# Three pinned queue orders around the norms: gate products and mask loads behind the power on GpSimd, gate weights' low parts behind the statistics on VectorE

## The chip, the core and the metric

The kernel runs on one core of one Trainium2 chip. The engines are called here as the profile calls them: PE is TensorE, DVE is VectorE, ACT is ScalarE, POOL is GpSimd, SP is SyncE, which issues most of the DMAs. The metric is the device time of one execution in microseconds (us).

## The reference

Two blocks run one after the other on 256 tokens of width 1024. The first has two layers, each with an attention, a short convolution and a state-space scan side by side, and it also carries 256 context tokens through its first layer. Its sublayers end in a gated norm of their output, which is added to the stream:

```python
y = jnp.concatenate([y_att, y_sc, y_ssd], axis=-1) @ p['w_out']
x = x + g1 * _rms_norm(y, p['g_post_mix'])
...
f = jnp.square(jax.nn.relu(h @ p['w_ff1'])) @ p['w_ff2']
return x + gate * _rms_norm(f, p['g_post_ffn'])
```

The second block has two layers, one with a dilated and one with a plain window attention, both masked to a band. Each layer ends like this:

```python
x = layer_norm(DEEPNORM_ALPHA * x + h, ln_g[i], ln_b[i])
gate = jax.nn.sigmoid((x @ ple_w_gate[i]).astype(jnp.float32))
x = x.astype(jnp.float32) + gate * (p[i] @ ple_w_proj[i]).astype(jnp.float32)
```

## The kernel before

The tokens lie in tiles of 128 partitions. `xt[0]` and `xt[1]` are the context's two tiles, `xt[2]` and `xt[3]` those of the stream; each is two halves of 512 columns. A tile's post-norm runs alone, and tiles go in pairs.

A matrix product in float32 is made of three PE matmuls of rounded parts (`mm3`, L212). `split` makes the parts: ACT casts the value to its high part (L226) and DVE, or for every second part of the activations POOL, subtracts it from the value to get the low part (L227). A weight comes by a DMA that SP issues into a tile `raw` (`wblk`, L180 in the profile), and `wh` and `wl` are its high and low parts; a few `raw` tiles go round, so a new DMA waits until an older tile's `wl` is made.

`rpow` (L167, L168) makes the factor of a norm on POOL, with two tiny instructions: an addition of epsilon, and the power −1/2. `postnorm` (L424 and after) squares and sums a tile's two halves on ACT (L431), multiplies the halves by the gate (L432: first half on POOL, second on DVE), calls `rpow`, and adds the product times the factor to the stream on DVE (L435). `normed` (L406, L410) does the next norm: squares on ACT, `rpow`, and a scaling `q` on DVE. `modulated` (L420, L424) transposes `q` on PE, scales the transposed tile `tp` on DVE, and splits it into the parts `u`.

`load_mask` (L1020 and after) loads the mask of a window attention in two halves, with a DMA that POOL's queue issues (L1023) and a cast on POOL (L1024) for each. `second` (L1229 and after) ends a layer of the second block: the out-projection's result is added to the stream (L1245), its statistics are taken (L1246) and joined (L1250), `rpow` makes the factor, two passes normalize it (L1253, L1254), PE transposes it (L1002), and the gate's product follows, with weights from `wblk`.

A scheduler decides the order of the instructions of each engine: it walks the traced program with a simulated timeline and takes what it expects to be ready first, within what the data and the buffers allow. An engine then runs its instructions in that order, one behind the other. Two helpers bind the scheduler. `keep_in_program_order` holds an instruction behind the one that was traced before it on its engine. `issue_after(x)` holds all that is traced inside it behind `x` on the engine of `x`.

Of the kernel before, what the change touches and what calls it, by code (L numbers as in the profile page):

```python
# [13 lines left out]
ALU = mybir.AluOpType  # L14
# [4 lines left out]
KT = D // P  # L19
# [45 lines left out]
def body(ctx, tc, A, out):  # L65
    nc = tc.nc
    PE, ACT, DVE, POOL, SP = nc.tensor, nc.scalar, nc.vector, nc.gpsimd, nc.sync
# [15 lines left out]
    def nm(s):  # L83
        count[0] += 1
        return f"{s}{count[0]}"
# [84 lines left out]
    def wblk(src, segs, k0=0, nk=KT, keep=0, tag="u"):  # L170

        W = sum(w for _, w in segs)
        per = min(1024 // W, nk)
        v = src.rearrange("(k p) n -> p k n", p=P)
        got = []
        for k in range(0, nk, per):
            r = raw.tile([P, 1024], F32, tag="raw", name=nm("raw"))[:, 0:per * W].rearrange("p (k n) -> p k n", k=per)
            o = 0
            for c0, w in segs:
                SP.dma_start(r[:, :, o:o + w], v[:, k0 + k:k0 + k + per, c0:c0 + w])  # L180
                o += w
            if k >= nk - keep:
                for q in range(per):
                    h, l = B(tag, F32R)[:, 0:W], B(tag, F32R)[:, 0:W]
                    split(r[:, q, :], h, l)
                    got.append((h, l))
                continue
            n = min(512 // W, per)
            for a in range(0, per, n):
                h = wh.tile([P, 512], F32R, tag="wh", name=nm("wh"))[:, 0:n * W]  # L190
                l = wl.tile([P, 512], F32R, tag="wl", name=nm("wl"))[:, 0:n * W]
                split(r[:, a:a + n, :].rearrange("p k n -> p (k n)"), h, l)
                for q in range(n):
                    got.append((h[:, q * W:(q + 1) * W], l[:, q * W:(q + 1) * W]))
        return got
# [86 lines left out]
    cols, halves = [None, None], [None, None]  # L282
# [144 lines left out]
    def postnorm(t, halves, gate):  # L427

        s2, rs, r = S(2), S(1), [R(), R()]
        for hf in range(2):  # L430
            ACT.activation(R(), halves[hf], AF.Square, scale=1.0 / 32, accum_out=s2[:, hf:hf + 1])  # L431
            (DVE if hf else POOL).tensor_tensor(r[hf], halves[hf], gate[hf], ALU.mult)  # L432
        rpow(rs, s2[:, 0:1], s2[:, 1:2], EPS)
        for hf in range(2):
            DVE.scalar_tensor_tensor(xt[t][hf], r[hf], rs, xt[t][hf], ALU.mult, ALU.add)  # L435
# [583 lines left out]
    def load_mask(n):  # L1019
        m = C([P, 5, 256], "c_mask", BF16, tag="c_tri")[:, 0:4, :].rearrange("p (s a) c -> p s (a c)", s=2)  # L1020
        for s in range(2):
            r = R()
            POOL.dma_start(r, A[n][:, s * 512:(s + 1) * 512])  # L1023
            POOL.tensor_copy(m[:, s, :], r)  # L1024
        return m

    def gated(po, z, pattern):
# [203 lines left out]
    def second(i, oT, pp, fill, done):  # L1231
        w_out = A["a_w_out_2" if i == 0 else "b_w_out_2"][0]
        lg, lb = [U(), U()], [U(), U()]
        for hf in range(2):
            brow(lg[hf], A["ln_g_2"][i, 512 * hf:512 * hf + 512])
            brow(lb[hf], A["ln_b_2"][i, 512 * hf:512 * hf + 512])
        st = [S(12), S(12)]
        hT, transpose = xT()
        for n in range(2):
            W = wblk(w_out, [(512 * n, 512)])  # L1240
            for t in range(2):
                x = xt[2 + t]
                ps = AN()
                mm3(ps, tok(oT, t, W))
                DVE.scalar_tensor_tensor(x[n], x[n], ALPHA, ps, ALU.mult, ALU.add)  # L1245
                DVE.bn_stats(st[t][:, 6 * n:6 * n + 6], x[n])  # L1246
        for t in range(2):
            x = xt[2 + t]
            mv, rs = S(2), S(1)
            DVE.bn_aggr(mv, st[t])  # L1250
            rpow(rs, mv[:, 1:2], None, LN_EPS)
            for n in range(2):
                DVE.scalar_tensor_tensor(x[n], x[n], mv[:, 0:1], lg[n], ALU.subtract, ALU.mult)  # L1253
                DVE.scalar_tensor_tensor(x[n], x[n], rs, lb[n], ALU.mult, ALU.add)  # L1254
            transpose(t)
        W = [wblk(A["ple_w_gate_2"][i], [(512 * n, 512)], keep=(0 if n else KT)) for n in range(2)]
        got = None
        for t in range(2):
            x = xt[2 + t]
            for n in range(2):  # L1260
                ps = AN()
                mm3(ps, tok(hT, t, W[n]))
                e = R()
                ACT.activation(e, ps, AF.Tanh, scale=0.5)
                DVE.scalar_tensor_tensor(e, e, 1.0, pp[t][n], ALU.add, ALU.mult)
                DVE.tensor_tensor(x[n], x[n], e, ALU.add)
                if i == 1:
                    SP.dma_start(out[0, t * P:(t + 1) * P, 512 * n:512 * n + 512], x[n])
            done(t)
            if t == 0:  # L1270
                got = fill()
        return got
# [97 lines left out]
```

## Time and profile before

| | us |
|---|---|
| median of three runs (lowest, highest) | 1543.17 (1542.04, 1545.42) |
| profiled execution, its own time | 1537.98 |
| its span | 1535.9 |
| PE busy in the span | 1470.2 (96%) |
| DVE busy | 1036.4 (67%) |
| ACT busy | 740.4 (48%) |
| POOL busy | 308.2 (20%) |
| mean granted clock of PE, share of full speed | 0.986 |

A time on the profile's timeline counts from the start of the span. PE is busy for all but 65.7 us of it, so a change of order can win only where PE stands, and it can lose wherever it makes PE stand longer.

### The profile page before, as it was taken

How to read it: one execution, taken by the hardware profiler on the slowest of the kernel's cores; microseconds unless marked ns; L12 is line 12 of the kernel's file. 1: busy time of each engine (PE TensorE's matmuls, PEld its weight loads, DVE VectorE, ACT ScalarE, POOL GpSimd, SP SyncE). 2: the span in 40 equal slices, each digit the busy share in tenths (PEclk: the TensorE clock that was granted, in tenths of full speed). 3: DMA queues.
4: the chain of work that ended last, by engine and by line, in shares of the span. 5: the costliest groups of instructions: out<-in, count | busy, mean ns of one | idle time of the engine just before them, and what ended most of it. 6: DMA issues, size and time to landing. Idle time of an engine off the chain costs nothing.

```text
span 1535.9 us, 23433 instructions
## 1 busy us (share of the span) xinstructions
PE 1470.2 (96%) x8417; PEld 1215.3 (79%) x8417; DVE 1036.4 (67%) x2057; ACT 740.4 (48%) x1594; POOL 308.2 (20%) x356
## 2 busy tenths in 40 slices
PE   6997999999999999998899899999999999999998
PEld 4766678888878888878797689997888889878886
DVE  3559556478597557478776756676876786567866
ACT  3433345564233333255556654565566457445663
POOL 1225201150001111034331301112310320021110
PEclk9998999999999999999999999999999999999999
DMA  9854622325366546334423546555436550645442
GB/s 294 266 182 153 219 84 88 97 66 195 123 219 206 180 152 200 109 83 135 132 76 117 165 139 213 188 195 169 153 107 203 162 179 15 219 139 180 138 149 69
DMA packets 131687, 236.51 MB, mean 154 GB/s; under 512 B 12624, under 2 KB 31251, under 8 KB 131571
## 3 DMA queue, kind: packets, MB, share of 16 engines
q1 hardware_dynamic: 130688, 233.46, 47.0%
q0 software_dynamic: 704, 1.50, 0.3%
q8 instruction: 66, 1.08, 0.3%
q14 instruction: 50, 0.41, 0.1%
q10 hardware_dynamic: 179, 0.06, 0.0%
HBM read 233.87 MB, written 1.11 MB: 153 GB/s over the span
## 4 chain that ended last, share of the span: by engine, by line
PE 84%; DVE 7%; DMA 4%; issue 2%; ACT 2%; POOL 1%; SPq 0%; ACTq 0%; DVEq 0%; POOLq 0%
PE sc L212 47%; PE mm L212 20%; PE tp L459 3%; DVE wl L227 2%; PE fl L303 2%; DMA raw<-in_w_mod_dram 1%; DMA raw<-in_ple_w_gate_dram 1%; PE fl L212 1%; DMA raw<-in_w_in_dram 1%; PE sc L793 1%; PE mm L639 1%; PE sc L1083 1%; PE sc L634 1%; DVE u L782 1%; PE sc L1108 1%
## 5 line engine op out<-in xcount | busy, mean ns | idle before, releaser
L227 DVE TENSOR_TENSOR wl<-raw,wh 128x512 fp32r<-128x512 f32 (+1 forms) x606 | 421.2, 731 | 141.1 <-ACT wh L226 138.1
L226 ACT CAST wh<-raw 128x512 fp32r<-128x512 f32 (+1 forms) x606 | 359.2, 620 | 307.0 <-PE sc L212 104.5
L212 PE MATMUL sc<-wh,u 128*128 128x512 f32 (+2 forms) x1424 | 458.6, 389 | 3.5 <-DVE r L505 2.0
L212 PEld LDWEIGHTS sc<-wh,u 128*128 128x128 f32 x1424 | 265.4, 189 | 58.8 <-ACT p L226 2.2
L212 PE MATMUL sc<-wl,u 128*128 128x512 f32 (+2 forms) x712 | 274.6, 387 | 0.1
L212 PE MATMUL sc<-u,wh 128*128 128x256 f32 (+1 forms) x1072 | 265.1, 336 | 1.8 <-ACT wh L226 1.1
L212 PE MATMUL mm<-wh,u 128*128 128x512 f32 (+1 forms) x648 | 219.3, 395 | 1.0 <-ACT u L226 1.0
L212 PEld LDWEIGHTS sc<-u,wh 128*128 128x128 f32 x1072 | 184.0, 191 | 24.5 <-issue 2.0
L212 PE MATMUL sc<-u,wl 128*128 128x256 f32 (+1 forms) x536 | 178.0, 335 | 0.0
L212 PEld LDWEIGHTS sc<-wl,u 128*128 128x128 f32 x712 | 134.6, 189 | 24.8 <-DVE wl L227 0.5
L949 POOL TENSOR_TENSOR r<-r 128x256 f32<-128x256 f32 (+1 forms) x60 | 64.3, 1073 | 420.1 <-ACT r L947 380.2
L212 PEld LDWEIGHTS mm<-wh,u 128*128 128x128 f32 x648 | 122.2, 190 | 26.1 <-ACT u L226 1.7
L212 PE MATMUL mm<-wl,u 128*128 128x512 f32 (+1 forms) x324 | 127.2, 393 | 0.0
L212 PE MATMUL mm<-u,wh 128*128 128x256 f32 (+1 forms) x512 | 117.6, 317 | 1.1 <-ACT wh L226 1.0
L212 PEld LDWEIGHTS sc<-u,wl 128*128 128x128 f32 x536 | 102.0, 191 | 9.6
L342 DVE SCALAR_TENSOR_TENSOR q<-raw,c_sT,q 128x512 f32<-128x512 f32 x112 | 85.0, 788 | 13.8 <-DMA raw<-in_w_mod_dram 13.2
L212 PEld LDWEIGHTS mm<-u,wh 128*128 128x128 f32 x512 | 86.1, 191 | 9.2 <-issue 1.7
L212 PE MATMUL mm<-u,wl 128*128 128x256 f32 (+1 forms) x256 | 80.4, 314 | 0.0
L950 DVE TENSOR_TENSOR u<-r,u 128x256 fp32r<-128x256 f32 (+1 forms) x60 | 33.6, 561 | 63.0 <-POOL r L949 60.7
L1016 POOL TENSOR_TENSOR r<-r,r 128x512 f32<-128x512 f32 (+1 forms) x30 | 44.6, 1491 | 151.4 <-DVE r L1014 151.3
L212 PEld LDWEIGHTS mm<-wl,u 128*128 128x128 f32 x324 | 61.5, 190 | 12.5 <-issue 0.8
L227 POOL TENSOR_TENSOR u<-r,u 128x256 fp32r<-128x256 f32 (+1 forms) x48 | 38.2, 801 | 119.3 <-ACT u L226 119.0
(318 smaller groups left out, 1984.7 us busy)
## 6 DMA issues: line engine op xcount, KB each, us to landing
raw<-in_w_ff_dram SPq DMA_DIRECT2D x128, 512.0 KB, 4.5
raw<-in_w_mod_dram SPq DMA_DIRECT2D x80, 512.0 KB, 4.5
raw<-in_a_w_in_dram SPq DMA_DIRECT2D x80, 512.0 KB, 3.9
raw<-in_w_in_dram SPq DMA_DIRECT2D x32, 512.0 KB, 5.1
raw<-in_b_w_in_dram SPq DMA_DIRECT2D x18, 512.0 KB, 4.6
raw<-in_w_mod_dram SPq DMA_DIRECT2D x32, 256.0 KB, 5.2
raw<-in_w_out_dram SPq DMA_DIRECT2D x16, 512.0 KB, 3.8
raw<-in_ple_w_gate_dram SPq DMA_DIRECT2D x16, 512.0 KB, 3.9
```

Of the source, the lines that this page charges most:

```text
L212: PE.matmul(ps, s, m, start=(i == 0), stop=(i == n - 1))
L226: ACT.copy(h, src)
L227: (eng or DVE).tensor_tensor(l, src, f(h), ALU.subtract)
L303: PE.matmul(ps[32 * g:32 * g + 32, :], sT[:, k + q, :], rs[g // per][:, q, w * (g % per):w * (g % per) + w], start=(k + q == 0), stop=(k + ...
L342: DVE.scalar_tensor_tensor(a, r[:, q, :], w, a, ALU.mult, ALU.add)
L459: PE.transpose(tp[:, b * P:(b + 1) * P], p[:, b * P:(b + 1) * P], ident)
L634: PE.matmul(ps[:, b * P:(b + 1) * P], qT[t][:, hs], kT[b][:, hs], start=True, stop=True, skip_group_check=True)
L639: PE.matmul(po[64 * e:64 * e + 64, hp * P:(hp + 1) * P], V[b // 2][:, 256 * (b % 2) + 64 * h:256 * (b % 2) + 64 * h + 64], pT[e][:, b * P: ...
L782: DVE.tensor_scalar(o, o, cs[:, t, c:c + 1], 0.0, ALU.subtract, ALU.min)
L949: POOL.tensor_tensor(f2[:, a:b], r[:, a:b], r[:, a:b], ALU.mult)
L950: DVE.tensor_tensor(l, f2[:, a:b], f(h), ALU.subtract)
L1016: POOL.tensor_tensor(a[:, 0:w], a[:, 0:w], b[:, 0:w], ALU.add)
```

## The change

It computes the same with the same instructions. Three places of the code bind the scheduler that did not before. The product on POOL of a `postnorm` is held behind what was traced before it on POOL: for the second tile of a pair that is the first tile's power, and for the first tile of the context's pair it is the last of the POOL subtractions of the stream's `modulated`. The mask's DMAs and casts are held in the order in which they are written, behind the power that was traced before them. In `second`, all that the gate's weights need on DVE is held behind the first tile's joined statistics.

```diff
--- before.py
+++ after.py
@@ -429,7 +429,10 @@
         s2, rs, r = S(2), S(1), [R(), R()]
         for hf in range(2):
             ACT.activation(R(), halves[hf], AF.Square, scale=1.0 / 32, accum_out=s2[:, hf:hf + 1])
-            (DVE if hf else POOL).tensor_tensor(r[hf], halves[hf], gate[hf], ALU.mult)
+            ins = (DVE if hf else POOL).tensor_tensor(r[hf], halves[hf], gate[hf], ALU.mult)
+            if hf == 0:
+
+                tc.keep_in_program_order(ins)
         rpow(rs, s2[:, 0:1], s2[:, 1:2], EPS)
         for hf in range(2):
             DVE.scalar_tensor_tensor(xt[t][hf], r[hf], rs, xt[t][hf], ALU.mult, ALU.add)
@@ -1020,8 +1023,8 @@
         m = C([P, 5, 256], "c_mask", BF16, tag="c_tri")[:, 0:4, :].rearrange("p (s a) c -> p s (a c)", s=2)
         for s in range(2):
             r = R()
-            POOL.dma_start(r, A[n][:, s * 512:(s + 1) * 512])
-            POOL.tensor_copy(m[:, s, :], r)
+            tc.keep_in_program_order(POOL.dma_start(r, A[n][:, s * 512:(s + 1) * 512]))
+            tc.keep_in_program_order(POOL.tensor_copy(m[:, s, :], r))
         return m
 
     def gated(po, z, pattern):
@@ -1244,16 +1247,20 @@
                 mm3(ps, tok(oT, t, W))
                 DVE.scalar_tensor_tensor(x[n], x[n], ALPHA, ps, ALU.mult, ALU.add)
                 DVE.bn_stats(st[t][:, 6 * n:6 * n + 6], x[n])
+        agg = []
         for t in range(2):
             x = xt[2 + t]
             mv, rs = S(2), S(1)
-            DVE.bn_aggr(mv, st[t])
+            ins = DVE.bn_aggr(mv, st[t])
+            agg.append(ins.ins)
             rpow(rs, mv[:, 1:2], None, LN_EPS)
             for n in range(2):
                 DVE.scalar_tensor_tensor(x[n], x[n], mv[:, 0:1], lg[n], ALU.subtract, ALU.mult)
                 DVE.scalar_tensor_tensor(x[n], x[n], rs, lb[n], ALU.mult, ALU.add)
             transpose(t)
-        W = [wblk(A["ple_w_gate_2"][i], [(512 * n, 512)], keep=(0 if n else KT)) for n in range(2)]
+
+        with tc.issue_after(agg[0]):
+            W = [wblk(A["ple_w_gate_2"][i], [(512 * n, 512)], keep=(0 if n else KT)) for n in range(2)]
         got = None
         for t in range(2):
             x = xt[2 + t]
```

Lines below L432 stand three lower after the change, those below L1250 four or five.

**POOL, out-projection of the first layer, the context's pair of tiles.** `r_3027` and `r_3066` are the two tiles' products, `s_3026` and `s_3065` their factors, `u_2611` a low part of the stream's activations. Before:

```order
L432 TENSOR_TENSOR r_3027<-u_2773,q_2637 128x512
L167 TENSOR_SCALAR s_3026<-s_3025 128x1
L432 TENSOR_TENSOR r_3066<-u_2800,q_2637 128x512
L168 TENSOR_TENSOR s_3026<-s_3026,c_mhalf_99 128x1
L167 TENSOR_SCALAR s_3065<-s_3064 128x1
L227 TENSOR_TENSOR u_2611<-r_2996,u_2610 128x256
L168 TENSOR_TENSOR s_3065<-s_3065,c_mhalf_99 128x1
```

After:

```order
L227 TENSOR_TENSOR u_2611<-r_2996,u_2610 128x256
L432 TENSOR_TENSOR r_3027<-u_2773,q_2637 128x512
L167 TENSOR_SCALAR s_3026<-s_3025 128x1
L168 TENSOR_TENSOR s_3026<-s_3026,c_mhalf_99 128x1
L432 TENSOR_TENSOR r_3066<-u_2800,q_2637 128x512
L167 TENSOR_SCALAR s_3065<-s_3064 128x1
L168 TENSOR_TENSOR s_3065<-s_3065,c_mhalf_99 128x1
```

The subtraction `u_2611` has come to the head, and the first tile's power now stands ahead of the second tile's product.

**ACT, the same place.** `s_3025` and `s_3064` gather the two tiles' squares, `sc_3000` is a half of the first tile, `u_2608` and `u_2610` are high parts of the stream's activations. Before:

```order
L431 ACTIVATE r_3029,s_3025<-u_2773 128x512
L431 ACTIVATE r_3032,s_3025<-sc_3000 128x512
L226 CAST u_2608<-r_2989 128x256
L431 ACTIVATE r_3068,s_3064<-u_2800 128x512
L431 ACTIVATE r_3071,s_3064<-sc_3039 128x512
L226 CAST u_2610<-r_2996 128x256
```

After:

```order
L431 ACTIVATE r_3029,s_3025<-u_2773 128x512
L226 CAST u_2608<-r_2989 128x256
L226 CAST u_2610<-r_2996 128x256
L431 ACTIVATE r_3032,s_3025<-sc_3000 128x512
L431 ACTIVATE r_3068,s_3064<-u_2800 128x512
L431 ACTIVATE r_3071,s_3064<-sc_3039 128x512
```

The two casts, of which `u_2610` feeds the subtraction `u_2611`, now stand ahead of the square of the first tile's second half. At the second layer's out-projection the cast `u_8101` and one of a weight have moved ahead of such a square in the same way, the subtraction `u_8101` ahead of the product on POOL, and two weight subtractions ahead of the tile's L435 on DVE.

**POOL, end of the second layer's feed-forward.** `r_10494` and `r_10536` are the products, `s_10493` and `s_10535` the factors, the rest is the first attention mask. Before:

```order
L432 TENSOR_TENSOR r_10494<-u_8757,q_8463 128x512
L167 TENSOR_SCALAR s_10493<-s_10492 128x1
L432 TENSOR_TENSOR r_10536<-u_8772,q_8463 128x512
L168 TENSOR_TENSOR s_10493<-s_10493,c_mhalf_99 128x1
L1023 DMA r_10585<-in_mask_a_dram 128x512
L1023 DMA r_10588<-in_mask_a_dram 128x512
L167 TENSOR_SCALAR s_10535<-s_10534 128x1
L168 TENSOR_TENSOR s_10535<-s_10535,c_mhalf_99 128x1
L1024 CAST c_mask_10584<-r_10585 128x512
L1024 CAST c_mask_10584<-r_10588 128x512
```

After:

```order
L432 TENSOR_TENSOR r_10494<-u_8757,q_8463 128x512
L167 TENSOR_SCALAR s_10493<-s_10492 128x1
L168 TENSOR_TENSOR s_10493<-s_10493,c_mhalf_99 128x1
L432 TENSOR_TENSOR r_10536<-u_8772,q_8463 128x512
L167 TENSOR_SCALAR s_10535<-s_10534 128x1
L168 TENSOR_TENSOR s_10535<-s_10535,c_mhalf_99 128x1
L1026 DMA r_10585<-in_mask_a_dram 128x512
L1027 CAST c_mask_10584<-r_10585 128x512
L1026 DMA r_10588<-in_mask_a_dram 128x512
L1027 CAST c_mask_10584<-r_10588 128x512
```

The first power stands ahead of the second product, and both mask DMAs stand behind both powers, the second of them behind the first cast.

**DVE, second layer norm of the second block.** `x_111` is a half of the first tile, `s_15524` its joined statistics, `wl_15625` and `wl_15629` low parts of gate weights. Before:

```order
L227 TENSOR_TENSOR wl_15625<-raw_15622,wh_15624 128x512
L227 TENSOR_TENSOR wl_15629<-raw_15622,wh_15628 128x512
L1245 SCALAR_TENSOR_TENSOR x_111<-x_111,mm_15470 128x512
L1246 BN_STATS s_15326<-x_111 128x6
L1250 BN_AGGR s_15524<-s_15326 128x2
L1253 SCALAR_TENSOR_TENSOR x_110<-x_110,s_15524,u_15318 128x512
```

After:

```order
L1248 SCALAR_TENSOR_TENSOR x_111<-x_111,mm_15470 128x512
L1249 BN_STATS s_15326<-x_111 128x6
L1254 BN_AGGR s_15524<-s_15326 128x2
L227 TENSOR_TENSOR wl_15625<-raw_15622,wh_15624 128x512
L227 TENSOR_TENSOR wl_15629<-raw_15622,wh_15628 128x512
L1258 SCALAR_TENSOR_TENSOR x_110<-x_110,s_15524,u_15318 128x512
```

The two subtractions have gone from ahead of the tile's last addition to behind its joined statistics. At the first layer norm they moved only behind the joined statistics, since the addition and its statistics stood ahead of them already.

## Rows read from the trace of the kernel before

**Rows 1.** The page: busy time of the engines, share, instructions.
```profile
PE 1470.2 (96%) x8417; PEld 1215.3 (79%) x8417; DVE 1036.4 (67%) x2057; ACT 740.4 (48%) x1594; POOL 308.2 (20%) x356
```

**Rows 2.** Timeline of PE: start, us, instructions, [idle before, releaser].
```profile
321.43 0.41 PE L420 MATMUL tp<-c_ident,q 128*128 128x128 f32 x2 [1.18 <-DVE q L410]
...
699.28 0.41 PE L420 MATMUL tp<-c_ident,q 128*128 128x128 f32 x2 [1.44 <-DVE q L410]
...
864.69 0.50 PE L212 MATMUL mm<-u,u 128*128 128x512 f32 x1 [1.33 <-DVE u L227]
...
1051.31 0.44 PE L985 MATMUL tp<-c_ident,x 128*128 128x128 f32 x2 [1.68 <-DVE x L435]
...
1371.63 0.55 PE L1002 MATMUL tp<-c_ident,x 128*128 128x128 f32 x3 [0.72 <-DVE x L1254]
...
1506.12 0.60 PE L1002 MATMUL tp<-c_ident,x 128*128 128x128 f32 x2 [1.13 <-DVE u L227]
```

**Rows 3.** Windows: stretch, length, busy us (count) by engine, PEclk, DMA share, GB/s.
```profile
1052.30:1055.70 3.40, 3.40 (x9) 2.53 (x9) 0.54 (x2) 0.02 (x1) 0.70 (x2) 0.50 0.02 7
1056.00:1059.40 3.40, 3.40 (x18) 2.75 (x17) 1.51 (x3) 2.03 (x5) 0.00 (x0) 1.00 0.00 0
```

**Rows 4.** Timeline of POOL, out-projection, second pair of tiles.
```profile
313.89 0.30 POOL L167 TENSOR_SCALAR s<-s 128x1 f32<-128x1 f32 x1
...
314.27 1.30 POOL L432 TENSOR_TENSOR r<-u,q 128x512 f32<-128x512 f32 x1
...
315.53 0.74 POOL L168 TENSOR_TENSOR s<-s,c_mhalf 128x1 f32<-128x1 f32 x1
...
317.28 1.10 POOL L227 TENSOR_TENSOR u<-r,u 128x256 fp32r<-128x256 f32 x1
```

**Rows 5.** Timeline of ACT, the same place.
```profile
312.27 0.58 ACT L431 ACTIVATE r<-sc 128x512 f32<-128x512 f32 x1
...
313.47 0.41 ACT L226 CAST u<-r 128x256 fp32r<-128x256 f32 x1 [0.53 <-DVE r L424]
```

**Rows 6.** Timeline of DVE, the same place.
```profile
318.93 1.42 DVE L435 SCALAR_TENSOR_TENSOR u<-r,s,u 128x512 f32<-128x512 f32 x2 [1.15 <-POOL s L168]
...
322.53 0.88 DVE L410 TENSOR_SCALAR q<-u,s 128x512 f32<-128x512 f32 x2 [0.69 <-POOL s L168]
```

**Rows 7.** Timeline of POOL, out-projection of the second layer.
```profile
861.57 1.01 POOL L168 TENSOR_TENSOR s<-s,c_mhalf 128x1 f32<-128x1 f32 x1
...
865.36 1.85 POOL L167 TENSOR_SCALAR s<-s 128x1 f32<-128x1 f32 x1 [2.77 <-ACT r L406]
```

**Rows 8.** Timeline of ACT, the same place.
```profile
860.83 2.18 ACT L226 CAST u<-raw 128x512 fp32r<-128x512 f32 x4
```

**Rows 9.** Timeline of POOL, end of the second layer's feed-forward.
```profile
1045.36 1.30 POOL L432 TENSOR_TENSOR r<-u,q 128x512 f32<-128x512 f32 x1
...
1046.62 1.00 POOL L168 TENSOR_TENSOR s<-s,c_mhalf 128x1 f32<-128x1 f32 x1
...
1047.58 1.17 POOL L1023 DMA_DIRECT2D r<-in_mask_a_dram  x2
```

**Rows 10.** Timeline of DVE, the same place.
```profile
1045.64 2.17 DVE L227 TENSOR_TENSOR wl<-raw,wh 128x512 fp32r<-128x512 f32 x2
...
1050.50 1.41 DVE L435 SCALAR_TENSOR_TENSOR x<-r,s,x 128x512 f32<-128x512 f32 x2 [0.77 <-POOL s L168]
```

**Rows 11.** Timeline of DVE, first layer norm of the second block.
```profile
1367.50 1.29 DVE L227 TENSOR_TENSOR wl<-raw,wh 128x512 fp32r<-128x512 f32 x2 [1.93 <-ACT wh L226]
...
1370.82 1.42 DVE L1254 SCALAR_TENSOR_TENSOR x<-x,s,u 128x512 f32<-128x512 f32 x2 [0.46 <-POOL s L168]
```

**Rows 12.** Timeline of DVE, second layer norm.
```profile
1497.74 1.29 DVE L227 TENSOR_TENSOR wl<-raw,wh 128x512 fp32r<-128x512 f32 x2 [3.62 <-ACT wh L226]
...
1500.64 1.41 DVE L1253 SCALAR_TENSOR_TENSOR x<-x,s,u 128x512 f32<-128x512 f32 x2
```

**Rows 13.** Timeline of SP's queue, second layer norm: DMA issues.
```profile
1499.07 6.46 SPq L180 DMA_DIRECT2D raw<-in_ple_w_gate_dram  x2
```


## The prediction

> **What bounds the kernel now.** I read the page's busy times first: PE works for 1470.2 us [rows 1] of a span of 1535.9 us, and DVE, the next engine, for 67% of it. So PE bounds the kernel, and only the 65.7 us in which it stands can be won. The next view is PE's timeline at the three pinned places, with what ended its waits. The reader is to see that at each of them PE does stand, for one or two microseconds, and waits for the end of a norm [rows 2]: for the scaled tile `q` (1.18 us at 321.43, 1.44 us at 699.28), for the stream `x` after a post-norm (1.68 us at 1051.31), for a normalized `x` (0.72 us at 1371.63), or for a low part `u` (1.33 us at 864.69, 1.13 us at 1506.12). Such a stop can cost more than itself: from 1052.3 to 1055.7 PE ran at a granted clock of 0.50, its lower level of 1.2 GHz, right after it had stood at 1051.31. It began 9 instructions there, against 18 in an equally long stretch at 1.00 soon after [rows 3]. Half of 3.4 us, 1.7 us, is what such a stretch costs.
>
> The third view is the timelines of POOL, ACT and DVE at each place, held against the new order. No instruction and no DMA is added or removed, so every term is a shift of the end of a norm.
>
> **What is the price of a product behind the power.** A product on POOL takes 1.30 us [rows 4], the power 0.74 us [rows 4] to 1.01 us [rows 7]. Before the change the second product stands between the first tile's addition of epsilon (over at 314.19) and its power (315.53), 1.3 us in all [rows 4]. The change takes these away from the first tile. But the product is still needed for the second tile, and it now starts when DVE starts the first tile's L435. What DVE and POOL do to each other at such a time is seen at the other product: two subtractions on DVE that start at 1045.64, while the product runs until 1046.66 [rows 9], take 2.17 us [rows 10], and a pair with no POOL work beside it 1.29 us [rows 11]. So 0.88 us go to the overlap. The other way round, POOL's tiny addition took 1.85 us at 865.36, beside a run of such subtractions on DVE [rows 7], where another took 0.30 us [rows 4]: 1.55 us. One of the two engines pays about a microsecond each time.
>
> The Trainium skill (SBUF — State Buffer, section "Who interferes with whom") has a rule that speaks against the change here: GpSimd and a VectorE instruction with two SBUF inputs share a port, and the one that issues first keeps it for its whole instruction while the other is fully blocked. By it the moved product would cost up to its whole length, 1.30 us, at each place, more than the 0.88 us of the row. The rows agree that one waits for the other; which of them gets the port first behind a power, no row of before shows.
>
> **First layer's out-projection.** Of its two pairs the first has no wait of PE's behind it, and counts as nothing: PE has matmuls of the other tokens to do there. In the context's pair POOL begins with `u_2611`, which needs the cast `u_2610`. On ACT that cast and the one ahead of it stand before the square that began at 312.27; the first of them could begin only at 313.47, since it waited for DVE [rows 5]. Two casts of 0.41 us end at about 314.3, the square of 0.58 us at about 314.9, where before it ended at 312.85. On POOL: `u_2611` from 314.3 (it took 1.10 us) to about 315.3, the first product to 316.6, the addition and the power 0.30 + 0.74 + 0.1 us between them to 317.7. Before, the power ended at 316.27 [rows 4]. The first tile is 1.4 us late although a product was taken out of its way, because two other things were put there. Behind this power come the second product and the second factor: 317.7 + 1.30 + 1.14 = 320.1, if nothing stops the product, against the 318.93 at which the second tile's L435 began upon its factor [rows 6]: 1.2 us late. If the product waits for the L435 pair, 1.42 us [rows 6], it is 2.6 us. Then `q`, which began at 322.53 upon its factor [rows 6], is as late, and PE has nothing else: it stood there already. I take the middle, **+1.9** (1.2 to 2.6).
>
> **First layer's feed-forward end.** The same two edits meet the same pattern in the context's pair, but here the new order also puts about 30 matmuls of the next layer ahead of the transposes for which PE waited 1.44 us [rows 2], and weight subtractions ahead of L435, so that raw tiles come free sooner. The gain is at most that wait, −1.4; the loss is at most what the first place loses, +2.6. The middle, rounded down since the matmuls cover a part: **+0.5**.
>
> **Second layer's out-projection.** `u_8101` and a weight's cast stand ahead of the square, which so waits for two casts. In the row of four the first began at 860.83 and each took a quarter of 2.18 us [rows 8], so the square ends about 862.2, the product 862.7, the power (1.01 us) about 864.0; before, it ended at 861.57 + 1.01 = 862.58 [rows 7]. So L435 is 1.4 us late. The two weight subtractions that now stand ahead of it fill part of this, and they are what PE waits for at 864.69, 1.33 us. Five matmuls also go ahead of the transposes. PE can thus break even or better, −0.5 as I bound it; the worst is L435's 1.4 us and another hold of POOL's addition of 1.55 us, +2.95. I take **+1.2**.
>
> **Second layer's feed-forward end, with the mask.** Here the edit does most of what it can: the power moves up to 1045.36, where the product began, and the mask's DMA issues, 1.17 us of POOL from 1047.58, leave the second factor's way [rows 9]. But on DVE the two subtractions, whose second ends at 1047.81, stand ahead of the first tile's L435 [rows 10], so that tile was not held by its power. The second was: L435 at 1050.50 waited 0.77 us for its factor [rows 10]. That wait, and with it the clock's 1.7 us, is the most that can be won: −2.5. Against it the second product now starts at about 1046.1 among DVE's subtractions. If it is put off to DVE's first L435 (about 1048), it ends near 1050, and with addition and power near 1051.4: 0.9 us late. Between −2.5 and +0.9 I take **+0.2**, since the row of 865.36 shows POOL as the one that waits behind subtractions. The mask itself is first used far later; its later DMA costs nothing here. The second mask's load stands behind a norm in both orders, and is free as well.
>
> **First layer norm.** The joined statistics no longer wait behind the two subtractions that begin at 1367.50 upon a cast, so POOL's factor is ready early and DVE's 0.46 us before L1254 [rows 11] goes. L1253 still waits behind them. PE's transposes come 0.46 us earlier at best, with the joining's own time at most 0.7: **−0.4** (−0.7 to 0).
>
> **Second layer norm.** The subtractions could begin at 1497.74, upon their cast, and ended at 1499.03; what lies between that and 1500.64 [rows 12], 1.6 us of addition and statistics, now goes ahead of them, partly into DVE's wait of 3.62 us. SP issues the next raw tile at 1499.07, as soon as they are over [rows 13]; it goes out up to 1.6 us later, and the casts and low parts behind it come later too. In return L1254 follows without its wait. Bounds: +1.6, and −2.8 if PE's 1.13 us [rows 2] and a slow stretch of 1.7 us go. I take **+0.4**.
>
> **The sum:** 1.9 + 0.5 + 1.2 + 0.2 − 0.4 + 0.4 = +3.8 us. The profiled execution took 1537.98 us, so it would take 1541.8; that execution is 5.2 us below the median of 1543.17, on which I put the same shift: **1547.0**. About 0.2%, 3.1 us, is what a measurement of this kernel can tell from no change.
>
> **The rivals.**
> *Absorbed.* The late factors are covered, since PE's order is rearranged with them: the 30 matmuls and the five take the place of the waits. With the lower bounds of the two places that have such matmuls: 1.9 − 1.4 − 0.5 + 0.2 − 0.4 + 0.4 = +0.2, 1543.4. For it: PE has much ready work at both. Against it: at 321.43 nothing covers.
> *Faster.* PE's stops at 1051.31 and 1506.12 become so short that the clock isn't lowered after them. It decides at the second product of the feed-forward's end: if POOL gets it done before DVE's first L435, −2.5 there, and with −2.5 at the second layer norm, −0.5 at the first, +1.2 at the out-projection and nothing elsewhere −4.3, 1538.9. For it: both DMA issues really leave. Against it: DVE's subtractions stand at just that time.
> *Locked.* Each moved product waits for a whole pair on DVE or makes it wait. It decides at the same instant, behind a power: the upper bounds 2.6 + 2.6 + 2.95 + 0.9 with −0.4 and 0.4 give +9, 1552.2. That is the skill's rule carried through, as far as rows have shown it.
>
> **Chances.** The forecast as worked out 0.36, absorbed 0.35, faster 0.19, locked 0.10. The forecast and locked are slower by over 0.2%: 0.46; same 0.35; faster 0.19. The range leaves out the locked case and a half of the faster one: 1540.0 to 1550.5.
>
> **What would show it.** In the changed profile the first tile's power in the context's pair should end near 317.7 on before's scale, about 1.4 us late, with PE's wait for `q` and those right behind it longer by 1.9 us in sum; the second product of each pair should lie beside L435, one of them stretched. At 1051 PE's wait should stay near 1.7 us and the clock should still fall behind it. The forecast is wrong if the product slips in beside DVE at no cost, if ACT makes the two casts without delaying the square, or if the transposes moved behind matmuls leave PE no wait at all.

## The result, and the profile after

The change made the kernel slower: 1551.21 us against 1543.17 (medians of five runs). The ratio on record is 1.0067 with an interval of 1.0051 to 1.0084, so 8 to 13 us; the quotient of the two medians, 1.0052, lies at its lower end. The forecast was slower too, but +3.8 us, and 1551.21 lies above the range. The profiled execution took 1551.21 us, its span is 1549.3 us, and on the page PE is the engine to look at [rows 1]:

```profile
PE 1475.2 (95%) x8417; PEld 1217.9 (79%) x8417; DVE 1039.6 (67%) x2057; ACT 740.9 (48%) x1594; POOL 302.4 (20%) x356
```

PE stands for 74.1 us instead of 65.7, and is busy for 5.0 us more with the same 8417 instructions. Where this happens is seen by cutting both traces at the same matmuls, counted along PE. The next two views are windows, columns as in [rows 3], each line a stretch: the first 65 us, the first layer's out-projection, its feed-forward's end with what follows, the second layer's out-projection, its feed-forward's end, and the two layer norms. Before:

```profile
4.54:70.11 65.57, 53.21 (x444) 38.44 (x444) 31.34 (x80) 26.20 (x65) 15.91 (x28) 0.97 0.93 304
310.21:345.42 35.21, 31.95 (x232) 29.71 (x231) 25.14 (x47) 21.69 (x56) 19.55 (x25) 0.95 0.15 50
670.28:790.18 119.90, 106.84 (x732) 96.03 (x730) 97.76 (x229) 65.78 (x169) 47.98 (x62) 0.96 0.34 103
853.30:910.18 56.88, 53.79 (x250) 42.49 (x250) 41.42 (x77) 33.57 (x72) 11.07 (x13) 0.97 0.47 149
1045.03:1090.31 45.28, 42.85 (x196) 34.46 (x195) 32.33 (x56) 22.62 (x45) 13.58 (x14) 0.96 0.47 141
1365.31:1415.40 50.09, 46.43 (x227) 37.68 (x225) 37.09 (x70) 24.93 (x54) 10.44 (x9) 1.00 0.44 149
1490.21:1530.44 40.23, 38.79 (x170) 31.12 (x168) 28.76 (x50) 14.14 (x29) 3.40 (x4) 0.96 0.28 92
```

After:

```profile
4.54:73.02 68.48, 52.64 (x444) 38.30 (x445) 31.19 (x80) 26.25 (x65) 16.01 (x28) 0.98 0.90 296
313.05:348.85 35.80, 31.37 (x233) 29.80 (x231) 24.90 (x47) 21.86 (x56) 18.53 (x25) 0.95 0.15 49
674.31:801.50 127.19, 109.35 (x732) 98.47 (x731) 100.25 (x231) 66.89 (x171) 47.60 (x63) 0.93 0.33 97
864.57:923.70 59.13, 55.67 (x250) 43.05 (x251) 41.78 (x77) 33.54 (x72) 9.86 (x13) 0.94 0.44 143
1058.57:1103.22 44.65, 42.86 (x196) 34.51 (x195) 32.47 (x56) 22.71 (x45) 14.07 (x14) 0.96 0.49 144
1378.23:1429.40 51.17, 47.86 (x227) 38.82 (x226) 36.79 (x70) 24.92 (x54) 9.59 (x9) 0.97 0.44 147
1504.20:1543.81 39.61, 38.05 (x170) 29.64 (x168) 28.53 (x50) 14.24 (x29) 2.62 (x4) 1.00 0.29 94
```

Length less PE's busy time is the time that PE stands. The first stretch is 2.9 us longer although no engine's order differs there; that is not the change, and it makes the two profiled spans 13.4 us apart where the timed ratio says about 10. Of the others one stands out, the third: 119.90 us became 127.19, +7.3. PE stands 17.84 us there instead of 13.06, and its clock is 0.93 instead of 0.96, which makes the same 732 matmuls 2.5 us longer. The out-projections have +0.6 and +2.25, the second feed-forward's end −0.6, the layer norms +1.1 and −0.6.

Over the first 240 matmuls of the third stretch (56.5 us, before 47.6) PE stands 12.1 us instead of 7.3, so all of its longer standing lies there. Its four largest waits from 688 to 730 us, by line (total, times, longest):

```profile
PE sc L212 <- ACT u L226: 2.5, 1, 2.5
PE mm L212 <- DVE wl L227: 2.3, 1, 2.3
PE tp L420 <- DVE q L410: 2.1, 2, 1.2
PE sc L212 <- ACT p L226: 1.9, 1, 1.9
```

Before, its wait for `q` there was 1.44 us [rows 2], it waited 1.0 us for a part `u`, and it did not wait for `wl` or `p`. POOL's timeline: the first line is the last low part of the stream's activations, the second the context's first product, which is now pinned behind it:

```profile
700.93 1.28 POOL L227 TENSOR_TENSOR u<-r,u 128x256 fp32r<-128x256 f32 x1 [3.82 <-ACT u L226]
702.18 1.61 POOL L432 TENSOR_TENSOR r<-u,q 128x512 f32<-128x512 f32 x1
...
704.97 0.85 POOL L168 TENSOR_TENSOR s<-s,c_mhalf 128x1 f32<-128x1 f32 x1
...
707.88 0.84 POOL L168 TENSOR_TENSOR s<-s,c_mhalf 128x1 f32<-128x1 f32 x1
```

In before the same product ran thus:

```profile
686.86 1.29 POOL L432 TENSOR_TENSOR r<-u,q 128x512 f32<-128x512 f32 x1
...
691.20 1.01 POOL L168 TENSOR_TENSOR s<-s,c_mhalf 128x1 f32<-128x1 f32 x1
...
694.08 1.01 POOL L168 TENSOR_TENSOR s<-s,c_mhalf 128x1 f32<-128x1 f32 x1
```

The stretch begins 4.03 us later in the changed kernel (674.31 against 670.28). With that taken off, the product starts at 698.15 instead of 686.86, eleven microseconds late, and the two powers end 9.6 us late. Part of this is the pin itself: before, the last low part of the stream came only behind the product, at 693.10. The rest is that this low part is late: POOL waits 3.82 us for it, and it needs ACT, DVE and in the end PE's last transposes of the stream. Why these are late, DVE's timeline shows:

```profile
683.65 0.99 DVE L424 TENSOR_SCALAR r<-tp,c_scale,c_mod 128x256 f32<-128x256 f32 x2
686.80 1.29 DVE L227 TENSOR_TENSOR wl<-raw,wh 128x512 fp32r<-128x512 f32 x2 [2.16 <-ACT wh L226]
688.01 0.54 DVE L424 TENSOR_SCALAR r<-tp,c_scale,c_mod 128x256 f32<-128x256 f32 x1
```

Before, it was:

```profile
679.48 1.61 DVE L424 TENSOR_SCALAR r<-tp,c_scale,c_mod 128x256 f32<-128x256 f32 x3
681.70 0.69 DVE L227 TENSOR_TENSOR wl<-raw,wh 128x512 fp32r<-128x512 f32 x1 [0.60 <-ACT wh L226]
682.30 0.54 DVE L424 TENSOR_SCALAR r<-tp,c_scale,c_mod 128x256 f32<-128x256 f32 x1
```

In before DVE scales three transposed tiles in one go and then takes the weight's subtraction, which waits 0.60 us for its cast. After, two tiles are scaled, then the pair of subtractions waits 2.16 us for its cast, and the third tile is queued behind: at 688.01, or 684.0 with the 4.03 us taken off, where before it was done by 681.09. With the stream's second product pinned, the scheduler put the weight's subtractions ahead of the third tile, and PE's last stream transposes 20 instructions further back. The cast itself waited for the weight's DMA:

```profile
686.15 1.14 ACT L226 CAST wh<-raw 128x512 fp32r<-128x512 f32 x2 [6.13 <-DMA raw<-in_w_in_dram]
```

That is 682.12 with the 4.03 us taken off, against 681.04 before, and the weights' DMAs issued just ahead of it go out 1.2 us later in the stretch (at 680.14, 5.8 us into it, against 674.93, 4.7 us into it).

### The profile page after: what moved, and what is told of

The parts are those of the page before. It is cut to its first block, busy times and chain, and to the rows that moved or that the text cites. A ratio compares the mean times of both kernels' runs of the same rounds, so it can differ in the third digit from the quotient of the medians.

```text
span 1549.3 us, 23422 instructions
## 1 busy us (share of the span) xinstructions
PE 1475.2 (95%) x8417; PEld 1217.9 (79%) x8417; DVE 1039.6 (67%) x2057; ACT 740.9 (48%) x1594; POOL 302.4 (20%) x356
## 5 line engine op out<-in xcount | busy, mean ns | idle before, releaser
L212 PE MATMUL sc<-wh,u 128*128 128x512 f32 (+2 forms) x1424 | 464.1, 393 | 4.8 <-ACT u L226 2.5
```

The lines of the kernel that those rows point to most:

```text
L212: PE.matmul(ps, s, m, start=(i == 0), stop=(i == n - 1))
```

## The experiments

All are compared with the kernel before on the same chip. Where the pins of the products differ, `postnorm` gets a parameter and the callers (the out-projection, L900, and the feed-forward, L968) say for which tile it holds; X is the stream's pair (tiles 2, 3), CTX the context's (0, 1):

```diff
-    def postnorm(t, halves, gate):
+    def postnorm(t, halves, gate, pin=False):
...
-            if hf == 0:
+            if hf == 0 and pin:
                 tc.keep_in_program_order(ins)
```

The diffs below show the pin as the callers give it, against the changed kernel; "no mask pin" and "no stats pin" mean that `load_mask` and `second` are as before the change. The length of the third stretch is from the windows view between the same two matmuls; before it is 119.90 us, in the changed kernel 127.19.

**e1_first_only**, no mask pin, no stats pin.

```diff
+ out-projection: pin = len(pair) == 1 or t == pair[0]
+ feed-forward:   pin = t == pair[0]
```

> Keeps of the change only the pin of the first tile's product of a pair (and of the last tile of the first block, which runs alone): the products that come to stand behind a low part of another pair's activations. Mask and gate weights as before. Theory of the anchor: the whole loss comes from these three places, because that low part needs PE's transposes of the other pair, which come late; the time is 7 to 11 us above before, with PE about 7 us later over the end of the first layer's feed-forward and about 2 us over the second layer's out-projection. Theory of the overlap (the prediction's): a product behind a power costs by lying among DVE's instructions, so this kernel has a small loss, 0 to 3 us.

Measured: 1.0007 (0.9996 to 1.0018); third stretch 119.49 us. The context's first product is about 5 us late there and PE loses nothing. The theory of the anchor, as I had put it, fell: late products alone are covered.

**e2_second_only**, no mask pin, no stats pin.

```diff
+ out-projection: pin = len(pair) > 1 and t == pair[1]
+ feed-forward:   pin = t == pair[1]
```

> Keeps only the pin of the second tile's product behind the first tile's power. Theory of the anchor: within 2 us of before, and at the end of the second layer's feed-forward PE is about as late as before the change. Theory of the overlap: 4 to 9 us above before, most of it in the two ends of the first layer's context pair.

Measured: 1.0027 (1.0016 to 1.0038), 4.2 us; third stretch 121.94 us. The anchor asked for at most 2 us. This is the lower edge of what the overlap asked for, and e1 and e2 together are far from the whole 0.67%.

**e3_mask_only**, no product pin, no stats pin:

```diff
+ out-projection: pin = False
+ feed-forward:   pin = False
```

> Keeps only the order of the mask's loads. Both theories: within 1 us of before; with the two DMA issues, 1.17 us, out of the second factor's way, PE's wait of 1.68 us for the second tile shrinks by 0.4 to 1.2 us. If the gain seen there in the changed kernel (0.6 us) belongs to the second product's pin instead, this kernel shows none of it.

Measured: 0.9993 (0.9979 to 1.0006). At the second feed-forward's end PE stands 0.84 us less (1.59 instead of 2.43), so the gain there is the mask's; e2, with the second product's pin and without the mask's order, has 2.65 us there.

**e4_stats_only**, no product pin, no mask pin:

```diff
+ out-projection: pin = False
+ feed-forward:   pin = False
```

> Keeps only the gate weights' subtractions behind the joined statistics. Both theories: between -1 and +2 us against before; the changed kernel's two layer norms together lost about 0.5 us, with about 1.7 us of it a stretch of lower clock after the first. If that stretch comes from this pin, it is seen here too; if it comes from the mask's or the products' pins, not.

Measured: 1.0002 (0.9991 to 1.0013). PE stands 0.8 us less at the first layer norm. A slow stretch of 1.2 us lies behind it, but also, with 1.4 us, in the profile of e9 below, whose order there is before's; so it isn't the pin's.

**e5_products**: all product pins, no mask pin, no stats pin.

```diff
+ out-projection: pin = True
+ feed-forward:   pin = True
```

> Both pins of the products (first and second tile of a pair), mask and gate weights as before. The two single pins cost +0.1% and +0.3%, the whole change +0.7%. If the loss is a joint effect of the two pins, in which the second tile's pin moves the transposes that the first tile's pin waits for, this kernel is 7 to 10 us above before, and PE loses about 7 us over the end of the first layer's feed-forward. If the missing part comes from the mask's or the gate weights' pins, it is 3 to 6 us above before, the sum of the two.

Measured: 1.0068 (1.0052 to 1.0084), third stretch 124.30 us. The products' pins carry the whole loss, and more than the sum of e1 and e2. The stretch is 4.4 us longer than before, not the 7 us that I had put, although every engine's order in it is that of the changed kernel, whose profile has 127.19; 1.4 of the 2.9 us between the two are standing and the rest clock.

**e6_ffn0_products**, no mask pin, no stats pin.

```diff
+ out-projection: pin = False
+ feed-forward:   pin = not last
```

> Both pins of the products, but at the end of the first layer's feed-forward alone. Joint effect at this place: 5 to 8 us above before, all of it there. If the loss is spread over the places, 1 to 3 us.

Measured: 1.0044 (1.0028 to 1.0059), third stretch 124.54 us: two thirds of the loss come from this place alone.

**e7_free_first**, mask and stats pins kept.

```diff
+ out-projection: pin = True
+ feed-forward:   pin = not (not last and t == 0)
```

> The whole change, without one pin: that of the first context tile's product at the end of the first layer's feed-forward. Theory of the moved anchor: the loss there falls from about 7 us to about 2, and the kernel is 2 to 5 us above before. If instead the second products among DVE's instructions are what costs there, it stays 7 us or more above before.

Measured: 1.0049 (1.0030 to 1.0067), 7.5 us (4.6 to 10.3) above before; third stretch 122.58 us, 4.6 us less than in the changed kernel. The stretch is as the moved anchor has it, but the time is not: that asked for 2 to 5 us, and 7 or more stood for the other reading. The interval holds both, so the timed runs of e7 decide nothing. PE still stands 15.09 us in the stretch.

**e8_mask_stats_last**, mask and stats pins kept.

```diff
+ out-projection: pin = False
+ feed-forward:   pin = last and t == pair[1]
```

> The change without its costly places: the mask's order, the gate weights' pin, and of the products' pins only that at the end of the second layer's feed-forward. Both theories: 0 to 3 us below before; if each of the single pins is as neutral as measured (0.9993 and 1.0002), not to be told from before.

Measured: 0.9999 (0.9986 to 1.0012). The change without its costly places is worth nothing that can be told.

Next, the pins at the third stretch are parted by pair, all without mask and stats pins. **e9_x2_c1**, **e10_c1_c2**, **e11_x2**, the out-projection unpinned in each:

```diff
+ e9:  feed-forward: pin = not last and (t == X[1] or t == CTX[0])
+ e10: feed-forward: pin = not last and t in CTX
+ e11: feed-forward: pin = not last and t == X[1]
```

> At the end of the first layer's feed-forward alone: pins of the stream's second product and of the context's first product. Theory of the moved anchor (the stream's pin makes the stream's last transposes late, the context's pin makes the first context factor wait for them): nearly the whole loss of both pins there, PE 3 to 5 us later over this place, the context's first product some 10 us later than before against the matmuls ahead of it, the time 4 to 8 us above before. Rival, that the two pins of the context's own pair add up (first product late, second behind the late power): under 2 us above before, product 5 us late as with the first pins alone.

> The same place, both pins of the context's pair, none on the stream's. Moved anchor: the anchor stays where it was, the first product is 5 us late as with the first pins alone, PE has matmuls to cover that, within 1.5 us of before. Rival, the context's own two pins add up: 4 to 8 us above before.

> The same place, the stream's second product alone. Both theories: the stream's last transposes and with them the context's chain 4 to 5 us late; PE loses what all second pins lost at this place, about 2 us; 1 to 5 us above before.

Measured: e9 1.0035 (1.0022 to 1.0048), stretch 122.37 us; e10 0.9986 (0.9976 to 0.9997), 116.66 us; e11 1.0015 (1.0001 to 1.0029), 123.58 us. The stretch in e10 and in e11:

```profile
674.44:791.10 116.66, 105.06 (x732) 94.98 (x731) 97.82 (x229) 65.82 (x169) 47.80 (x62) 0.97 0.35 106
674.93:798.51 123.58, 108.42 (x731) 97.57 (x730) 96.93 (x231) 66.46 (x171) 46.78 (x63) 0.94 0.33 100
```

So PE stands 11.60 us in e10 and 15.16 in e11, against 13.06 before: the stream's pin alone, with no pin on the context's pair, already makes it stand longer. In e9 and e10 the stretch begins at nearly the same time (674.65 and 674.44), so their timelines can be laid side by side. The first lines of DVE, then of POOL, in e9:

```profile
684.01 0.99 DVE L424 TENSOR_SCALAR r<-tp,c_scale,c_mod 128x256 f32<-128x256 f32 x2
686.95 1.29 DVE L227 TENSOR_TENSOR wl<-raw,wh 128x512 fp32r<-128x512 f32 x2 [1.96 <-ACT wh L226]
688.16 0.54 DVE L424 TENSOR_SCALAR r<-tp,c_scale,c_mod 128x256 f32<-128x256 f32 x1
```

```profile
699.94 1.28 POOL L227 TENSOR_TENSOR u<-r,u 128x256 fp32r<-128x256 f32 x1 [3.81 <-ACT u L226]
701.18 1.61 POOL L432 TENSOR_TENSOR r<-u,q 128x512 f32<-128x512 f32 x1
```

And in e10:

```profile
683.64 1.61 DVE L424 TENSOR_SCALAR r<-tp,c_scale,c_mod 128x256 f32<-128x256 f32 x3
685.65 0.69 DVE L227 TENSOR_TENSOR wl<-raw,wh 128x512 fp32r<-128x512 f32 x1 [0.39 <-ACT wh L226]
686.25 0.54 DVE L424 TENSOR_SCALAR r<-tp,c_scale,c_mod 128x256 f32<-128x256 f32 x1
```

```profile
694.24 1.13 POOL L227 TENSOR_TENSOR u<-r,u 128x256 fp32r<-128x256 f32 x1 [3.38 <-ACT u L226]
695.33 1.61 POOL L432 TENSOR_TENSOR r<-u,q 128x512 f32<-128x512 f32 x1
```

With the stream's pin the third scaled tile is again queued behind a wait for a cast (1.96 us), the last low part comes at 699.94 and the context's first product at 701.18. Without it the three are scaled in one go, and the product starts at 695.33, 5.6 us earlier in its stretch, although it is pinned behind the same low part. Both pins on the context's pair add nothing. The rival falls. In e9's profile the clock did not fall as often as in e6's, so its stretch is shorter; the standing, 16.19 and 16.75 us, is nearly the same. That the context's first pin adds to the stream's is seen less clearly: the timed intervals of e9 and e11 overlap, and PE stands 1.0 us longer in e9.

**e12_anchor_earlier**: e6 with the stream's last odd low part made on VectorE in that call of `modulated`.

```diff
-def modulated(xn, kind, scale, shift, dst, ks=range(KT), o=0):
+def modulated(xn, kind, scale, shift, dst, ks=range(KT), o=0, pool=(1, 3, 5, 7)):
...
-            split(r[:, 0:w], h, l, POOL if k % 2 else DVE)
+            split(r[:, 0:w], h, l, POOL if k in pool else DVE)
...
+        modulated(..., pool=(1, 3, 5) if pair == X else (1, 3, 5, 7))
```

> The same place, both pins on both pairs, but the stream's last low part is made on VectorE instead of GpSimd, so that the pin of the context's first product falls on the low part before it, whose transposes come about 4.5 us earlier. Moved anchor: the context's first product starts 3 to 5 us earlier than with all pins there, and the loss at this place falls from about 4.5 us to 2 or less. If the product is late for another reason, its accumulated sums or the subtractions beside it, it starts no more than 1 us earlier and the loss stays.

Measured: 1.0016 (1.0001 to 1.0032) against e6's 1.0044; stretch 122.05 us against 124.54. POOL's timeline:

```profile
696.78 0.74 POOL L227 TENSOR_TENSOR u<-r,u 128x256 fp32r<-128x256 f32 x1 [4.54 <-ACT u L226]
697.48 1.48 POOL L432 TENSOR_TENSOR r<-u,q 128x512 f32<-128x512 f32 x1
701.44 0.99 POOL L167 TENSOR_SCALAR s<-s 128x1 f32<-128x1 f32 x1 [2.49 <-ACT r L431]
```

The product follows its new anchor at 697.48; e6 has it at 700.18 in a stretch that began 3.14 us earlier (673.11 against 676.25), so it comes 6 us earlier. The power gains less, since its addition now waits 2.49 us for the square. In the profiles the stretch is 2.15 us longer than before instead of 4.6, and PE stands 15.61 us instead of 16.75, not much more than in e11. The timed intervals just overlap.

**e13_whole_without_x2**, mask and stats pins kept.

```diff
+ out-projection: pin = True
+ feed-forward:   pin = last or t != X[1]
```

> The whole change without one pin: that of the stream's second product at the end of the first layer's feed-forward. If this pin is what makes the anchor late, the whole change loses its largest part with it: 0 to 4 us above before, where the whole change was 8 to 10. If the loss is a sum over all places, it is 6 us or more above before.

Measured: 1.0015 (1.0000 to 1.0029), third stretch 119.92 us, as before. Without this one pin some three quarters of the change's loss are gone.

**e14_outproj_only**, no mask pin, no stats pin.

```diff
+ out-projection: pin = len(pair) > 1
+ feed-forward:   pin = False
```

> The pins of the products at the first layer's out-projection alone, where the prediction saw its largest term, +1.9 us. By that working: 1 to 3 us above before, PE standing 1.2 to 2.6 us longer there. By the traces so far, about 1.2 us of longer standing there.

Measured: 0.9994 (0.9980 to 1.0007). In the profile PE stands 1.1 us longer there (36.43 us with 32.10 busy, against 35.21 with 31.95); the timed runs don't show it, −0.9 us (−3.1 to +1.1), where the working asked for 1 to 3.

**e15_candidate**, mask and stats pins kept, and **e16_c1_c2_again**, the kernel of e10.

```diff
+ e15: feed-forward: pin = (last and t == X[1]) or (not last and t in CTX)
+ e15: out-projection: pin = False
```

> What the runs so far point to: both pins of the context's pair at the first layer's feed-forward (0.9986 alone), the pin at the second layer's feed-forward, the mask's order and the gate weights' pin (0.9999 together). If these add up: 1 to 4 us below before. If the 0.9986 was chance, no difference.

> The kernel with both pins of the context's pair at the first layer's feed-forward, a second time. If its gain is real: again 1 to 3 us below before. If it was chance: within 1 us.

Measured: e15 0.9986 (0.9974 to 0.9999), e16 0.9992 (0.9979 to 1.0006). The best of what the pins can do is some 0.1%, about what a measurement can tell; e10's 0.9986 was not repeated in full, and I don't count it as a gain.

**All profiles of the third stretch together**, cut at the same matmuls:

| pinned there | kernels | PE stands, us | context's first product starts, us into the stretch |
|---|---|---|---|
| neither of the two | before, e3, e4, e8, e14 | 11.5 to 13.1 | 16.4 to 16.9 |
| context's first | e1, e10, e13, e15, e16 | 11.6 to 13.3 | 20.9 to 21.9 |
| stream's second | e2, e7, e11 | 15.1 to 15.2 | 21.2 to 22.7 |
| both | changed kernel, e5, e6, e9 | 16.2 to 17.8 | 26.4 to 27.9 |

Before, e3, e4 and e8 have one and the same order there, so 1.2 us is what profiles differ by without a cause in the order. A product that is four to five microseconds late costs PE nothing in the second line; about as late, it stands beside 2.0 to 3.7 us of longer standing in the third. So the greater part comes with the stream's pin itself and not by the late product; the context's pin behind it adds 1.0 to 2.8 us. That the pins cost more in a row than apart also holds by the timed runs: e10 and e11 add up to 1.0001, give or take 0.0018 (their intervals added in quadrature), and e6's interval begins at 1.0028. Of the stream's part 0.9 us lies in the first 60 matmuls, right behind its late tile (3.3 us of standing in e11, 2.4 before); how much of it is the tile's place in the queue, how much the later DMAs and how much PE's own new order, no run parts.

## Why the prediction was wrong

The direction was right, in part by luck: half of the forecast's +3.8 us lay at the first out-projection, where the timed runs of e14 show no loss. The step that failed is the term **"First layer's feed-forward end", +0.5** (at most +2.6): "The same two edits meet the same pattern in the context's pair". It measured +7.3 us in the profile, 4.8 of standing and 2.5 of clock; 4.4 to 4.6 us in the profiles of e5 and e6, 3.3 to 3.7 of them standing; and the pins of this place alone cost 6.8 us (4.3 to 9.1) in the timed runs of e6. Two things were wrong in it.

It looked at the context's pair alone, and put the stream's pair at nothing without a reason. The stream's second product, pinned there, runs beside the first tile's L435 pair (line 438 now) and makes it take 2.44 us (at 671.90, just ahead of the stretch) instead of 1.41 (at 669.19 before); weight subtractions and their late cast come ahead of the third scaled tile, and that tile is 3.4 us late. This alone makes PE stand 2.0 to 3.7 us longer. The term also had raw tiles come free sooner; the weights' DMAs from the fifth to the 35th microsecond of the stretch, counted one by one, go out 0.4 to 4.9 us later.

And it took the anchor, the last low part of the stream, only as an instruction that stands ahead of the context's first product, and not as one that has to be able to run. With the stream's tiles late, the anchor is 5.5 us later in e9 than in e10, and the product with it. PE's matmuls covered the product's first five microseconds (e1, e10), but not the next five: another 1.0 to 2.8 us of standing.

**The wait behind a power.** I had the second product put off at the second feed-forward's end, and so its term at +0.2. It ran there at once:

```profile
1058.90 0.55 POOL L168 TENSOR_TENSOR s<-s,c_mhalf 128x1 f32<-128x1 f32 x1
1059.43 1.58 POOL L432 TENSOR_TENSOR r<-u,q 128x512 f32<-128x512 f32 x1
1061.10 1.14 POOL L167 TENSOR_SCALAR s<-s 128x1 f32<-128x1 f32 x1
```

```profile
1059.17 2.38 DVE L227 TENSOR_TENSOR wl<-raw,wh 128x512 fp32r<-128x512 f32 x2
...
1062.08 2.73 DVE L438 SCALAR_TENSOR_TENSOR x<-r,s,x 128x512 f32<-128x512 f32 x4
```

The two subtractions beside it took 2.38 us, 0.2 more than with the product beside them before [rows 10], and the four L435 (line 438 now) ran without a wait. PE stands 0.6 us less: by e3 the mask's two DMA issues, gone from the second factor's way, bring 0.84, and by e2 the product's pin takes 0.2. The forecast named this gain's place and took it back. The clock fell there as before, 0.96 in both views, as forecast.

**First out-projection, +1.9.** Right in part, and nearer to its lower bound: the first tile's power ends at 317.43 on before's scale (317.7 was forecast), and PE stands 1.2 us longer (4.43 instead of 3.26 in the second line of the two windows views), 1.1 in e14. The second tile's L435 began 1.5 us late (323.27, less the 2.84 us by which this stretch begins later, against 318.93 [rows 6]), where I had 1.2 for a product that nothing stops. But this is the price of the two casts and the subtraction that went ahead of the first product, not of the product behind the power: with the first product's pin alone (e1) PE stands 4.47 us there, with the second's alone (e2) 2.57. The product's own price was paid by DVE:

```profile
319.71 0.56 POOL L168 TENSOR_TENSOR s<-s,c_mhalf 128x1 f32<-128x1 f32 x1
320.23 1.30 POOL L432 TENSOR_TENSOR r<-u,q 128x512 f32<-128x512 f32 x1
...
322.33 0.84 POOL L168 TENSOR_TENSOR s<-s,c_mhalf 128x1 f32<-128x1 f32 x1
```

```profile
320.31 2.44 DVE L438 SCALAR_TENSOR_TENSOR u<-r,s,u 128x512 f32<-128x512 f32 x2 [1.84 <-POOL s L168]
...
323.27 1.40 DVE L438 SCALAR_TENSOR_TENSOR u<-r,s,u 128x512 f32<-128x512 f32 x2
```

The product started behind the power at 320.23 and took its 1.30 us; the L435 pair started at 320.31 and took 2.44 us instead of 1.42 [rows 6]. The Trainium skill (SBUF — State Buffer, section "Who interferes with whom") says that the order of issue decides which of the two blocks; the rows agree: the one that began 0.08 us earlier was not slowed, the other lost 1.0 us. By e2 PE did not wait for it here.

**Second out-projection, +1.2.** PE stands 0.4 us longer. The other 1.9 us of that stretch are its clock, 0.94 instead of 0.97. No run has these pins alone. In the working the square ends at 862.5 (860.83, two casts of 0.545 and 0.58), not 862.2; the sum is the same, since the product ends later, at 862.7.

**First layer norm, −0.4.** PE stands 0.35 us less, as worked out, 0.8 in e4; a slow stretch of 1.4 us that before's profile did not have hides it. **Second layer norm, +0.4.** PE stands 0.1 us longer; the clock stayed at 1.00 there where before it fell, −0.7 us. The standing of both is within the bounds, and the timed runs of e4 and e8 see neither.

**The rivals.** Absorbed holds for e1 and e10, not for the whole. Faster fell: nothing wins more than a microsecond. Locked gave about the time, +9, 1552.2, but not the cause: a moved product did make an L435 pair wait 1.0 us, at the first out-projection and in the stream's pair at the first feed-forward's end, which Locked didn't name; none was itself held for a whole pair, and at the first out-projection PE did not wait for it.

## What to carry to other kernels

An order pin is only as good as its anchor: before one instruction is held behind another, follow that other back to what it waits for, through every engine, and see what else the same change moves in that chain. Pins that cost little one by one can stand in a row; so cost them together, or time them together and apart, and count the pair ahead as well as the pair in question. Where a scheduler re-plans around a pin, the difference of the orders on the other engines, DVE's here, tells more than the pinned queue itself.

## What the runs showed of the hardware that I had not expected

The clock's slow stretches behind a stop of PE are not a property of the order alone. At the second feed-forward's end e4 has before's order on every engine, and PE stands as long (2.44 us; before 2.43), but its clock stayed up:

```profile
1051.22:1094.95 43.73, 41.29 (x196) 33.38 (x195) 32.51 (x55) 22.64 (x45) 13.31 (x14) 1.00 0.48 146
```

It is 1.55 us shorter than the fifth line of before's windows. One kernel does both: the stretch took 45.26 us at 0.96 in e10 and 43.69 at 1.00 in e16. So I had no ground to count 1.7 us of clock for or against an edit from one profile: a difference of one such stretch between two profiled executions is not evidence. The timed runs are, and the standing is where it differs by more than the 1.2 us by which it varies at one and the same order.
